# A hybrid decoder layer on one core: 128-row attention scores, both chunks of the triangular inverse doubled in common, and an instruction planner that prices row changes

## The chip, the cores and the metric

The kernel runs on one core of a Trainium2 chip. A time is what the device takes for one execution, in microseconds (us); the median over several executions counts. The profile comes from one more execution, whose own time stands beside its span. The engines are called PE (TensorE, matmuls), DVE (VectorE), ACT (ScalarE), POOL (GpSimd) and SP (SyncE, which issues the DMAs).

## The reference

One decoder layer, float32, 256 tokens of width 1024. `x` is RMS-normalised and multiplied by one weight matrix of 1024 x 4104. Half of the columns feed eight softmax heads of 64, the other half four heads of 128 of a gated delta rule; both results are gated, concatenated, multiplied by `w_out`, normalised and added to `x`:

```python
h = rms_norm(x, norm_pre_w)
a_q, a_k, a_v, a_z, d_q, d_k, d_v, d_z, d_b, d_a = split(h @ w_in)
moba_out = moba_attention(a_q, a_k, a_v) * silu(a_z)       # causal, ALiBi, 8 heads of 64
g_q, g_k, g_v = split(silu(causal_conv4(concat(d_q, d_k, d_v))))
o = gated_delta_rule(g_q, g_k, g_v, g, beta)               # 4 heads of 128
gdn_out = rms_norm(o, gdn_norm_w) * silu(d_z)
return x + rms_norm(concat(moba_out, gdn_out) @ w_out, norm_post_w)
```

In the delta rule each chunk of tokens needs the inverse of a unit lower triangular matrix, `(I + A)^-1`, where `A` holds products of keys times decays.

## The kernel before

**Tiling.** Tokens are two tiles of 128 (`t` = 0, 1; for the delta rule these are its two chunks). Every projection is a product of float32 split in two float32r parts (`hi`, `lo`), three matmuls in place of one: `hi*hi + hi*lo + lo*hi`. The transposed input is `hhi`, `hlo`. A weight group (`dk`, `dq`, `dv`, `av`, `aq`, `ak`, `az`; 512 columns) comes in two DMAs of 1 MB into four `raw` buffers; ACT writes `..._hi` (a copy that rounds), DVE writes `..._lo` (the subtraction); PE runs 96 matmuls on each group.

**The first stage, `dz`** (lines 427 to 441 and 629 to 641). `x` comes in four DMAs of half rows, the weights of `d_z`, `d_b`, `d_a` (520 columns) in four DMAs of two of the eight k-slices. `dz_piece(1)` multiplies the right 264 columns for all k-slices, then `dz_piece(0)` the left 256. `d_b` and `d_a` lead to the gates `bet`, `gneg`. `ps_warm` matmuls on zeros fill PE while nothing else can run (`WARM`, flagged `late`).

**The gates' decay matrices** (692 to 703). Per chunk a bank `ps_d` gets a mask (`ident16` times `far16`, bf16) and then, head by head, `gs` (DVE: `strl` times the head's gate) times `triu`, in float32.

**The inverse** (stages `inv` and `dbl`, 769 to 875). `bT` is the transposed `A` of four heads. Diagonal blocks of 16 are solved by a loop of 15 steps on DVE (`wprod`, `wc`) for both chunks together. `dbl` then goes from blocks of 16 to 32, 64 and 128. It holds the transposed inverse `wT` and the inverse `xX`. Per chunk and level PE makes `ps_y` (from `bT` and `xX`), ACT copies it to `yz`, PE makes `ps_w` (subtracted from `wT` by DVE) and, at the first two levels, `ps_x` (subtracted from `xX`). At level 32 these matmuls use 32 rows of the array, at level 64 they use 64, and `ps_x` at level 16 uses 64 and 32; `ps_y` and `ps_w` at level 16 use all 128.

**The recurrence** (`rec`, 906 to 959): for chunk 0 `ps_p` from `wT` and `vt`, the state `ps_S`, the output `ps_o`; then chunk 1 with the state (`ps_kS`, `ps_qS`, `ps_p`, `ps_o`). `mixd` transposes the result for the output projection.

**Attention** (979 to 1032). Per head the scores go into a bank `ps_s` of 128 + 256 columns: queries of tile 0 against keys of tile 0 in plain float32 (`qa`, `ka`), queries of tile 1 against all keys in three float32r matmuls (`qa_h`, `qa_l`, `ka_h`, `ka_l`). A head has 64 features, so these matmuls use 64 rows; two heads of a pair lie in the two halves. Softmax on DVE and ACT, `ps_pt` transposes, `ps_av` multiplies by the values.

**The order.** Nothing runs as written. Each call is recorded (`record`, 149) with its reads and writes and a modelled `cost` (197); `run` (227) plays a list schedule over the engines, eight rounds, and `emit` (348) issues each engine's instructions in that order. So each engine's queue is fixed in advance, and PE runs what stands next in its queue. What decides between ready operations is a rank, moved per stage by `LEAD`; `SLACK` is the window on PE in which the rank decides; `LAT` the time from one engine to another. The model before knows that a matmul may use fewer rows (`work`) but has no price for going from one row range to another.

Of the kernel before, what the change touches and what calls it, by code (L numbers as in the profile page):

```python
# [111 lines left out]
class Op:  # L112
    __slots__ = ("n", "eng", "call", "args", "kw", "cost", "table", "preds", "succs", "bufs", "start", "end", "pin", "late", "boost", "work", "load", "pass_", "stage")
# [10 lines left out]
class Plan:  # L124
# [24 lines left out]
    def record(self, eng, real, name, args, kw):  # L149
# [16 lines left out]
        op.work = op.load = op.pass_ = 0.0  # L166
        if eng == "pe":
# [5 lines left out]
            k = views[1].box[0][1] - views[1].box[0][0]  # L173
            op.work = k / P
# [22 lines left out]
    def cost(eng, name, views, kw):  # L197
# [26 lines left out]
        row = (v.box[-1][1] - v.box[-1][0]) * 4  # L224
        return max(400, (v.box[0][1] - v.box[0][0]) * v.size() * 4 / (240 if v.box[1][1] - v.box[1][0] == KT // 2 else 330))

    def run(self, rank, banks, reverse=False):
# [26 lines left out]
        table, load, last = None, 1.0, 0.0  # L254
        window, done, cold, share, self.low = 0, {}, True, 1.0, 1.0
        for _ in range(len(ops)):
            best = None
            for e, todo in ready.items():
                cand = []
                for op in todo:  # L260
                    t = max(at[op], free[e])
                    if e == "pe":
                        t = max(t, last + op.load)
                    else:
                        t = max([t] + [b.held for b in op.bufs if b.tag is None])
# [6 lines left out]
                if not cand:  # L272
# [3 lines left out]
                    (c for c in cand if c[0] <= t0 + (SLACK if e == "pe" else 1)),  # L276
                    key=lambda c: (-1e9 if c[1].pin else 1e9 if c[1].late else rank[c[1]] - c[1].boost 
# [101 lines left out]
LEAD = {"out0": 3258, "dk": 2097, "inv": -1876, "av": 6719, "out1": -9380, "att0": -470, "mixd": -508}  # L379
WARM = 36  # L380
# [3 lines left out]
def tile_hybrid(  # L384
# [44 lines left out]
    dz_raw = [plan.tile(sb, [P, KH, GROUP + 2 * HG], F32, f"raw_dz{i}", tag="raw", bufs=RAW_BUFS) for i in range(2)]  # L429
    HD = D // 2  # L430
    for t in range(NT):
        for c0 in (0, HD):
            SP.dma_start(xs[t][:, c0 : c0 + HD], x[0, t * P : (t + 1) * P, c0 : c0 + HD], pin=True)
        if t == 0:
            SP.dma_start(wcol, norm_pre_w[0].rearrange("(p kt) -> p kt", kt=KT), pin=True)
    for k in range(0, KT, 2):
        SP.dma_start(dz_raw[k // KH][:, k % KH : k % KH + 2, :], w_cols[:, k : k + 2, 3584:], pin=True)
# [170 lines left out]
    def token_piece(raw, n, name, fine):  # L608

        banks = [bank([P, n], f"ps_{name}_{t}") for t in range(NT)]  # L610
        kn = 2 if n > 2 * PIECE - 1 else KH
        for kg in range(0, KT, kn):
# [3 lines left out]
            for k in range(kn):  # L616
                for t in range(NT):
                    ts = slice(t * P, (t + 1) * P)
                    kt = kg + k
                    PE.matmul(banks[t], hhi[:, kt, ts], hi[:, k, :], start=(kt == 0), stop=False)  # L620
                    PE.matmul(banks[t], hhi[:, kt, ts], lo[:, k, :], start=False, stop=False)
                    PE.matmul(banks[t], hlo[:, kt, ts], hi[:, k, :], start=False, stop=(kt == KT - 1))
# [5 lines left out]

    def dz_piece(half):
        n = PIECE + 2 * HG * half  # L630
        banks = token_piece(lambda k, m: dz_raw[k // KH][:, k % KH : k % KH + m, PIECE * half : PIECE * half + n],
                            n, f"dz{half}", 2)
        for t in range(NT):
            if half:
                V.tensor_copy(ba[:, t, :], banks[t][:, PIECE:])
            A.activation(zt[t][:, 2 * half : 2 * half + 2, :].rearrange("p h d -> p (h d)"), banks[t][:, :PIECE], AF.Silu)

    plan.stage = "dz1"
    dz_piece(1)
    plan.stage = "dz0"  # L640
    dz_piece(0)


# [46 lines left out]
    PE.matmul(pc.rearrange("p t h -> p (t h)"), triu, gneg.rearrange("p t h -> p (t h)"), start=True, stop=True)  # L690
    A.activation(egc, pc, AF.Exp, scale=-1.0)
    for t in range(NT):
# [122 lines left out]

    for t in range(NT):
        ns = sl(f"ms{t}", HB, f"ns{t}")
        V.tensor_tensor(ns, bT[t], lvl.rearrange("p n two s -> p (n two s)")[:, None, :].to_broadcast(HB), OP.mult)
        yz = sl(f"yz{t}", HB, f"yz{t}")
        G.memset(yz, 0.0)  # L820
        py = bank([P, HG, 64], f"ps_y16_{t}")
        for h in range(HG):
            PE.matmul(py[:, h, :], ns[:, h, :], half_cols(xX[t], 0, h), start=True, stop=True)
        A.activation(half_cols(yz, 0).sized(256), py.rearrange("p h (n s) -> p h n s", n=n), AF.Copy)
        pw = bank([P, HG, 64], f"ps_w16_{t}")
        for h in range(HG):
            PE.matmul(pw[:, h, :], yz[:, h, :], half_cols(wT[t], 1, h), start=True, stop=True)

        px = bank([P, HG, 2 * BASE], f"ps_x16_{t}")
        for b, nb in ((0, 2), (4 * BASE, 1)):  # L830
            r = slice(b, b + 2 * BASE * nb)

            def first(m, h=slice(None)):
                v = m[r, h, r]
                if h == slice(None):
                    return v.rearrange("p h (n two s) -> p h n two s", n=nb, two=2)[:, :, :, 0, :].sized(HG * BASE * nb)
                return v.rearrange("p (n two s) -> p n two s", n=nb, two=2)[:, :, 0, :]

            for h in range(HG):
                PE.matmul(px[r, h, : BASE * nb], wT[t][r, h, r], first(yz, h), start=True, stop=True)  # L840
            x_ = first(xX[t])
            V.tensor_tensor(x_, x_, px[r, :, : BASE * nb].rearrange("p h (n s) -> p h n s", n=nb), OP.subtract)
# [4 lines left out]
    for t in range(NT):
        py = bank([P, HG, L], f"ps_y32_{t}")
        pw = bank([P, HG, L], f"ps_w32_{t}")
        px = bank([P, HG, L], f"ps_x32_{t}")  # L850
        yz = sl(f"yz{t}", [P, HG, L], f"yz32_{t}")
        halves = [(slice(b, b + L), slice(b + L, b + 2 * L)) for b in range(0, P, 2 * L)]
        for r1, r2 in halves:
            for h in range(HG):
                PE.matmul(py[r2, h, :], bT[t][r1, h, r2], xX[t][r1, h, r1], start=True, stop=True)
            A.activation(yz[r2], py[r2], AF.Copy)
        for b, (r1, r2) in enumerate(halves):
            for h in range(HG):
                PE.matmul(pw[r1, h, :], yz[r2, h, :], wT[t][r2, h, r2], start=True, stop=True)
            if b == 0:  # L860
                for h in range(HG):
# [281 lines left out]
```

## Time and profile before

| | |
|---|---|
| median of 3 runs | 182.91 us (182.87 to 187.65) |
| profiled execution, own time | 183.36 us |
| its span in the profile | 181.6 us, mean granted PE clock 0.988 |
| PE busy | 171.3 us, 1351 instructions |
| DVE, ACT, POOL busy | 134.5, 104.6, 16.7 us |
| DMA | 24.91 MB, 137 GB/s on the mean |

Times inside the profile count from the first instruction. Every row carries line 366, the helper that issues all operations, so groups are told apart by tile names, read as output<-inputs. A PE row gives a matmul's start and its duration with the pipeline's latency; the pace of a stream is the distance from start to start. A plain float32 matmul shows as two records (two passes), a float32r matmul or a transpose as one. Both types are written `f32` in PE rows.

### The profile page before, as it was taken

Reading aid. Unit: us, or ns where it says so; the run is one execution under the profiler, and the core shown is the slowest. Engines: PE = TensorE matmul, PEld = TensorE weight load, DVE = VectorE, ACT = ScalarE, POOL = GpSimd, SP = SyncE. Lnnn points to the kernel's source line nnn. Section 1 sums busy time; section 2 is a strip of 40 time slices with the busy share of each in tenths; the row PEclk is TensorE's granted clock in tenths of the full one; section 3 lists DMA queues with packets and bytes.
Section 4 is the critical chain, followed back from the end, with each engine's and each line's share of the span. In section 5 each row is a group of like instructions: output and inputs, shape, how many; then the busy total and the mean of one; then the engine's idle time right before and its main releaser. Section 6 shows DMA issues by size and latency. Waiting matters only on the chain.

```text
span 181.6 us, 3546 instructions
## 1 busy us (share of the span) xinstructions
PE 171.3 (94%) x1351; PEld 155.8 (86%) x1351; DVE 134.5 (74%) x343; ACT 104.6 (58%) x231; POOL 16.7 (9%) x52
## 2 busy tenths in 40 slices
PE   6897999999999999999999999999999999999950
PEld 3585999999999978999999888898899998888850
DVE  3485969998599998594997787889885467962452
ACT  4486797393972948446643837745283488841130
POOL 8700000000030000400000000000000460000110
PEclk9999999999999999999999999999999999999995
DMA  5659799909955450625693515000000005500033
GB/s 154 247 206 304 230 277 296 368 23 253 277 166 128 122 216 14 216 84 220 195 391 78 196 13 218 0 5 0 5 0 4 0 0 137 213 0 0 0 115 115
DMA packets 12549, 24.91 MB, mean 137 GB/s; under 512 B 709, under 2 KB 1014, under 8 KB 12534
## 3 DMA queue, kind: packets, MB, share of 16 engines
q1 hardware_dynamic: 12534, 24.71, 43.0%
q8 instruction: 10, 0.16, 0.3%
q14 instruction: 5, 0.04, 0.1%
HBM read 23.65 MB, written 1.05 MB: 136 GB/s over the span
## 4 chain that ended last, share of the span: by engine, by line
PE 81%; DMA 7%; issue 4%; ACT 2%; SPq 2%; DVE 1%; POOLq 0%; POOL 0%; DVEq 0%; ACTq 0%
PE ps_out L366 9%; PE ps_av L366 8%; PE ps_az L366 7%; PE ps_ak L366 7%; DMA raw_dz<-in_w_in_dram 7%; PE ps_aq L366 6%; PE ps_dk L366 6%; PE ps_dq L366 6%; PE ps_dv L366 5%; PE ps_dz L366 5%; PE ps_s L366 4%; PE ps_pt L366 2%; PE ps_gb L366 2%; PE ps_y L366 2%; PE ps_w L366 2%
## 5 line engine op out<-in xcount | busy, mean ns | idle before, releaser
L366 DVE TENSOR_TENSOR o_lo<-raw_o,o_hi 128x1024 fp32r<-128x1024 f32 x8 | 9.8, 1222 | 2.6 <-ACT o_hi L366 2.6
L366 PE MATMUL ps_dz<-dz_hi,hhi 128*128 128x264 f32 (+1 forms) x32 | 9.3, 294 | 0.8 <-ACT dz_hi L366 0.8
L366 PE MATMUL ps_dz<-dz_lo,hhi 128*128 128x264 f32 (+1 forms) x32 | 9.4, 296 | 0.6 <-DVE dz_lo L366 0.6
L366 ACT ACTIVATE att_y<-att_y,mx 128x128 f32<-128x128 f32 (+1 forms) x16 | 7.1, 446 | 4.8 <-DVE mx L366 4.6
L366 PE MATMUL ps_az<-hlo,az_hi 128*128 128x256 f32 x32 | 9.8, 305 | 0.0
L366 ACT ACTIVATE o_hi<-raw_o 128x1024 fp32r<-128x1024 f32 x8 | 8.4, 1054 | 2.1 <-PE ps_out L366 2.1
L366 PE MATMUL ps_ak<-hlo,ak_hi 128*128 128x256 f32 x32 | 9.6, 300 | 0.0
L366 PE MATMUL ps_az<-hhi,az_lo 128*128 128x256 f32 x32 | 9.6, 303 | 0.0
L366 PE MATMUL ps_az<-hhi,az_hi 128*128 128x256 f32 x32 | 9.6, 300 | 0.0
L366 PE MATMUL ps_ak<-hhi,ak_lo 128*128 128x256 f32 x32 | 9.4, 299 | 0.0
L366 PE MATMUL ps_ak<-hhi,ak_hi 128*128 128x256 f32 x32 | 9.4, 293 | 0.0
L366 PE MATMUL ps_dq<-hhi,dq_lo 128*128 128x256 f32 x32 | 9.2, 287 | 0.0
L366 PE MATMUL ps_dq<-hlo,dq_hi 128*128 128x256 f32 x32 | 9.2, 286 | 0.0
L366 PE MATMUL ps_dq<-hhi,dq_hi 128*128 128x256 f32 x32 | 9.2, 286 | 0.0
L366 PE MATMUL ps_aq<-hhi,aq_hi 128*128 128x256 f32 x32 | 9.1, 284 | 0.0
L366 PE MATMUL ps_aq<-hhi,aq_lo 128*128 128x256 f32 x32 | 9.0, 282 | 0.0
L366 PE MATMUL ps_dk<-hlo,dk_hi 128*128 128x256 f32 x32 | 9.0, 281 | 0.0
L366 PE MATMUL ps_dk<-hhi,dk_hi 128*128 128x256 f32 x32 | 9.0, 281 | 0.0
L366 PE MATMUL ps_dv<-hlo,dv_hi 128*128 128x256 f32 x32 | 9.0, 281 | 0.0
L366 PE MATMUL ps_dv<-hhi,dv_hi 128*128 128x256 f32 x32 | 9.0, 280 | 0.0
L366 PE MATMUL ps_dv<-hhi,dv_lo 128*128 128x256 f32 x32 | 8.9, 280 | 0.0
L366 PE MATMUL ps_aq<-hlo,aq_hi 128*128 128x256 f32 x32 | 8.9, 284 | 0.0
(262 smaller groups left out, 634.2 us busy)
## 6 DMA issues: line engine op xcount, KB each, us to landing
raw_o<-in_w_out_dram SPq DMA_DIRECT2D x4, 1024.0 KB, 5.2
raw_dz<-in_w_in_dram SPq DMA_DIRECT2D x4, 520.0 KB, 9.3
raw_dk<-in_w_in_dram SPq DMA_DIRECT2D x2, 1024.0 KB, 12.0
raw_dq<-in_w_in_dram SPq DMA_DIRECT2D x2, 1024.0 KB, 9.0
raw_dv<-in_w_in_dram SPq DMA_DIRECT2D x2, 1024.0 KB, 7.5
raw_av<-in_w_in_dram SPq DMA_DIRECT2D x2, 1024.0 KB
raw_aq<-in_w_in_dram SPq DMA_DIRECT2D x2, 1024.0 KB, 6.1
raw_ak<-in_w_in_dram SPq DMA_DIRECT2D x2, 1024.0 KB, 6.8
```

The costliest lines, as they stand in the source:

```text
L366: op.call(*args, **kw)
```

## The change

All parts are made at once.

- **Scores over 128 rows.** `qz[m]` holds a pair's queries, `hi` and `lo`, once with the other head's 64 rows zero for each head; both query tiles go in three float32r matmuls over 128 rows. `qa` and `ka` are gone; POOL writes the zeros.
- **Inverse.** Both chunks share tiles and banks at each level. `ps_x` is gone: `xX` is made from `wT` by a DVE transpose of 32 x 32 blocks (two more of 128 x 512, one of 32 x 256).
- **Gates.** `gs` is one DVE multiplication per chunk, followed by one float32 matmul of 512 columns, with the mask matmul behind it.
- **First stage.** `x` in two DMAs, the weights in eight of one k-slice; each pair of slices is split once, for all 520 columns, and used by both halves.
- **Planner.** It prices a change of row range at 90 ns (`SWITCH`), adds a `MARGIN` between engines, has new DMA prices, `LEAD` values and `WARM`. Its order is new throughout.

The diff, cut to its core:

```diff
@@ record / cost / run
+            op.rows = views[1].box[0]
-        return max(400, ... / (240 if v.box[1][1] - v.box[1][0] == KT // 2 else 330))
+        return max(400, n / (350 if v.box[-1][1] - v.box[-1][0] > 520 else 230))
-                t = max(t, p.end + self.LAT[a.eng][b.eng])
+                t = max(t, p.end + self.LAT[a.eng][b.eng]
+                        + (0 if a.eng == "pe" == b.eng else MARGIN[2 if a.eng == "dma" else 0 if b.eng == "pe" else 1]))
-                        t = max(t, last + op.load)
+                        t = max(t, last + op.load, free[e] + SWITCH * (op.rows != rows))
-                    (c for c in cand if c[0] <= t0 + (SLACK if e == "pe" else 1)),
+                    (c for c in cand if c[0] <= t0 + (SLACK + SWITCH if e == "pe" else 1)),
+SWITCH = 90
+BATCH = 0
+MARGIN = [411, 175, 0]
-LEAD = {"out0": 3258, "dk": 2097, "inv": -1876, "av": 6719, "out1": -9380, "att0": -470, "mixd": -508}
-WARM = 36
+LEAD = {"out0": 3258, "dk": 2097, "inv": -3594, "av": 2525, "dbl": -402, "out1": -1204, "att0": -470, "mixd": -508, "az": -1375}
+WARM = 48
@@ first stage
+    for t in range(NT):
+        SP.dma_start(xs[t], x[0, t * P : (t + 1) * P, :], pin=True)
+    for k in range(KT):
+        SP.dma_start(dz_raw[k // KH][:, k % KH, :], w_cols[:, k, 3584:], pin=True)
...
+    for q in range(KT // 2):
+        zh, zl = hl_tiles([P, 2, NZ], f"dz{q}")
+        for k in range(2):
+            split_into(dz_raw[2 * q // KH][:, 2 * q % KH + k, :], zh[:, k, :], zl[:, k, :])
+        for k in range(2):
+            for t in range(NT):
+                token_mms(z1[t], zh[:, k, PIECE:], zl[:, k, PIECE:], kt, t, st, sp)
+            for t in range(NT):
+                token_mms(z0[:, t, :], zh[:, k, :PIECE], zl[:, k, :PIECE], kt, t, ...)
@@ gates
-        PE.matmul(pd, ident16, far16[:, None, :].to_broadcast(HB), start=True, stop=False)
-        for h in range(HG):
-            V.tensor_scalar(gs[:, h, :], strl, gneg[:, t, h : h + 1], None, op0=OP.mult)
-            PE.matmul(pd[:, h, :], gs[:, h, :], triu, start=False, stop=h == HG - 1)
+        V.tensor_tensor(gs, triu[:, None, :].to_broadcast(HB), gneg[:, t, :, None].to_broadcast(HB), OP.mult)
+        PE.matmul(pd, strl, gs, start=True, stop=False)
+        PE.matmul(pd, ident16, far16[:, None, :].to_broadcast(HB), start=False, stop=True)
@@ dbl, level 32 (levels 16 and 64 likewise over NH = 8 heads)
+    for r1, r2 in halves:
+        for h in range(NH):
+            PE.matmul(py[r2, h, :], bTa[r1, h, r2], xXa[r1, h, r1], start=True, stop=True)
+        A.activation(yz[r2], py[r2], AF.Copy)
+    for b, (r1, r2) in enumerate(halves):
+        for h in range(NH):
+            PE.matmul(pw[r1, h, :], yz[r2, h, :], wTa[r2, h, r2], start=True, stop=True)
+        V.tensor_tensor(wTa[r1, :, r2], wTa[r1, :, r2], pw[r1], OP.subtract)
+        if b == 0:
+            V.transpose(xXa[r2, :, r1], wTa[r1, :, r2])
@@ attention
+    for q in qz[:3]:
+        for e in range(2):
+            G.memset(q[DA * (1 - e) : DA * (2 - e), :, e, :].bitcast(F32), 0.0)
+                A.activation(qh, ps[b, c, :], AF.Copy, scale=qs_)
+                V.scalar_tensor_tensor(ql, ps[b, c, :], qs_, qh, op0=OP.mult, op1=OP.subtract)
-                PE.matmul(ps_s[:, :P], qa[b, m, :], ka[b, m, :], start=True, stop=True)
-                PE.matmul(ps_s[:, P:], qh[b, m, :], kh[b, m, :], start=True, stop=False)
-                ...
+                for o, ts, ks in ((ps_s[:, :P], slice(0, P), slice(0, P)), (ps_s[:, P:], slice(P, T), slice(0, T))):
+                    PE.matmul(o, qh[:, ts], kh[:, m, ks], start=True, stop=False)
+                    PE.matmul(o, qh[:, ts], kl[:, m, ks], start=False, stop=False)
+                    PE.matmul(o, ql[:, ts], kh[:, m, ks], start=False, stop=True)
```

More of the change, by code (lines that the diff above doesn't have):

```diff
@@ L112 @@
 class Op:
-    __slots__ = ("n", "eng", "call", "args", "kw", "cost", "table", "preds", "succs", "bufs", "start", "end", "pin", "late", "boost", "work", "load", "pass_", "stage")
+    __slots__ = ("n", "eng", "call", "args", "kw", "cost", "table", "preds", "succs", "bufs", "start", "end", "pin", "late", "boost", "work", "load", "pass_", "stage", "rows")
 class Queue:
@@ L166, in record @@
         op.work = op.load = op.pass_ = 0.0
+        op.rows = None
         if eng == "pe":
@@ L171, in record @@
             op.pass_ = n / RATE.get(dt, 2.4) + 2.5
-            k = views[1].box[0][1] - views[1].box[0][0]
-            op.work = k / P
+            op.rows = views[1].box[0]
+            op.work = (op.rows[1] - op.rows[0]) / P
         op.preds, op.succs, op.bufs = {}, [], []
@@ L223, in cost @@
         v = views[0]
-        row = (v.box[-1][1] - v.box[-1][0]) * 4
-        return max(400, (v.box[0][1] - v.box[0][0]) * v.size() * 4 / (240 if v.box[1][1] - v.box[1][0] == KT // 2 else 330))
+        n = (v.box[0][1] - v.box[0][0]) * v.size() * 4
+        return max(400, n / (350 if v.box[-1][1] - v.box[-1][0] > 520 else 230))
     def run(self, rank, banks, reverse=False):
@@ L253, in run @@
         bank_free = [(0.0, i) for i in range(BANKS)]
-        table, load, last = None, 1.0, 0.0
+        table, load, last, rows = None, 1.0, 0.0, None
         window, done, cold, share, self.low = 0, {}, True, 1.0, 1.0
@@ L291, in run @@
             c = op.cost
+            if op.eng == "pe":
+                rows = op.rows
             if op.eng == "pe" and not reverse:
@@ L428, in tile_hybrid @@
     GROUP = 2 * PIECE
-    dz_raw = [plan.tile(sb, [P, KH, GROUP + 2 * HG], F32, f"raw_dz{i}", tag="raw", bufs=RAW_BUFS) for i in range(2)]
     HD = D // 2
+    NZ = GROUP + 2 * HG
+    dz_raw = [plan.tile(sb, [P, KH, NZ], F32, f"raw_dz{i}", tag="raw", bufs=RAW_BUFS) for i in range(2)]
     for t in range(NT):
[L432 to L437, printed above, removed]
+        SP.dma_start(xs[t], x[0, t * P : (t + 1) * P, :], pin=True)
+    SP.dma_start(wcol, norm_pre_w[0].rearrange("(p kt) -> p kt", kt=KT), pin=True)
+    for k in range(KT):
+        SP.dma_start(dz_raw[k // KH][:, k % KH, :], w_cols[:, k, 3584:], pin=True)
     SP.dma_start(sv[0:48, :], conv_w[0].rearrange("j (c p) -> (j c) p", p=P), pin=True)
@@ L457, in tile_hybrid @@
         PE.matmul(pz[:, :256], wz[:, :P], wz[:, :256], start=True, stop=True, late=True)
+    HB = [P, HG, P]
+    NH = NT * HG
+    HBB = [P, NH, P]
+    of_chunk = [slice(t * HG, (t + 1) * HG) for t in range(NT)]
+    yz16 = sl("yz", HBB, "yz")
     ident = const([P, P], "ident")
@@ L606, in proj_group, with token_mms, token_piece @@
         return pss
-    def token_piece(raw, n, name, fine):
+    def token_mms(o, hi, lo, kt, t, first, last):
+        ts = slice(t * P, (t + 1) * P)
+        PE.matmul(o, hhi[:, kt, ts], hi, start=first, stop=False)
+        PE.matmul(o, hhi[:, kt, ts], lo, start=False, stop=False)
+        PE.matmul(o, hlo[:, kt, ts], hi, start=False, stop=last)
+    def token_piece(raw, n, name, kn, fine):
         banks = [bank([P, n], f"ps_{name}_{t}") for t in range(NT)]
-        kn = 2 if n > 2 * PIECE - 1 else KH
         for kg in range(0, KT, kn):
@@ L617, in token_piece @@
                 for t in range(NT):
[L618 to L622, printed above, removed]
+                    token_mms(banks[t], hi[:, k, :], lo[:, k, :], kg + k, t, kg + k == 0, kg + k == KT - 1)
         return banks
@@ L627, in tile_hybrid @@
     ba = const([P, NT, 2 * HG], "ba")
[L629 to L641, printed above, removed]
+    z1 = [bank([P, PIECE + 2 * HG], f"ps_dz1_{t}") for t in range(NT)]
+    z0 = bank([P, NT, PIECE], "ps_dz0")
+    for q in range(KT // 2):
+        plan.stage = "dz"
+        zh, zl = hl_tiles([P, 2, NZ], f"dz{q}")
+        for k in range(2):
+            split_into(dz_raw[2 * q // KH][:, 2 * q % KH + k, :], zh[:, k, :], zl[:, k, :])
+        for k in range(2):
+            kt = 2 * q + k
+            st, sp = kt == 0, kt == KT - 1
+            for t in range(NT):
+                token_mms(z1[t], zh[:, k, PIECE:], zl[:, k, PIECE:], kt, t, st, sp)
+            for t in range(NT):
+                token_mms(z0[:, t, :], zh[:, k, :PIECE], zl[:, k, :PIECE], kt, t, st and t == 0, sp and t == NT - 1)
+    plan.stage = "dz"
+    for t in range(NT):
+        V.tensor_copy(ba[:, t, :], z1[t][:, PIECE:])
+        A.activation(zt[t][:, 2:4, :].rearrange("p h d -> p (h d)"), z1[t][:, :PIECE], AF.Silu)
+    A_ = [zt[t][:, 0:2, :].rearrange("p h d -> p (h d)") for t in range(NT)]
+    for t in range(NT):
+        A.activation(A_[t], z0[:, t, :], AF.Silu)
     vh = const([P, NT, HA * DA], "vh", F32R)
@@ L814, in half_cols, with head_cols @@
+    def head_cols(m, i, h):
         return m[:, h, :].rearrange("p (n two s) -> p n two s", n=n, two=2)[:, :, i, :]
+    nsa = sl("ms", HBB, "ns")
     for t in range(NT):
[L817 to L842, printed above, removed]
@@ L843, in tile_hybrid @@
-        hc = half_cols(wT[t], 1).sized(256)
-        V.tensor_tensor(hc, hc, pw.rearrange("p h (n s) -> p h n s", n=n), OP.subtract)
-    L = 2 * BASE
[L847 to L861, printed above, removed]
-                    PE.matmul(px[r2, h, :], wT[t][r2, h, r2], yz[r2, h, :], start=True, stop=True)
-                V.tensor_tensor(xX[t][r2, :, r1], xX[t][r2, :, r1], px[r2], OP.subtract)
-            V.tensor_tensor(wT[t][r1, :, r2], wT[t][r1, :, r2], pw[r1], OP.subtract)
@@ L865, in tile_hybrid @@
[L865 to L875 removed]
+        V.tensor_tensor(nsa[:, of_chunk[t], :], bT[t],
+                        lvl.rearrange("p n two s -> p (n two s)")[:, None, :].to_broadcast(HB), OP.mult)
@@ L878, in tile_hybrid @@
+    H = P // 2
+    yz = sl("yz", [P, NH, H], "yz64")
+    py = bank([P, NH, H], "ps_y64")
+    for h in range(NH):
+        PE.matmul(py[H:, h, :], bTa[:H, h, H:], xXa[:H, h, :H], start=True, stop=True)
+    A.activation(yz[H:], py[H:], AF.Copy)
+    pw = bank([P, NH, H], "ps_w64")
+    for h in range(NH):
+        PE.matmul(pw[:H, h, :], yz[H:, h, :], wTa[H:, h, H:], start=True, stop=True)
+    V.tensor_tensor(wTa[:H, :, H:], wTa[:H, :, H:], pw[:H], OP.subtract)
     plan.stage = "dq"
```

98 lines of the change are left out of this document (50 added, 48 removed).

## The prediction

> **What bounds the kernel now.** I read the page first, then the time by stretches, the chain that ended last, and the order of time on PE where row ranges mix. The page's busy times and the chain:
>
> ```profile
> PE 171.3 (94%) x1351; PEld 155.8 (86%) x1351; DVE 134.5 (74%) x343; ACT 104.6 (58%) x231; POOL 16.7 (9%) x52
> PE 81%; DMA 7%; issue 4%; ACT 2%; SPq 2%; DVE 1%; POOLq 0%; POOL 0%; DVEq 0%; ACTq 0%
> ```
>
> PE carries 81% of the chain. The table by stretches has the stretch in us and its length, then for PE, weight loads, DVE, ACT and POOL the busy time and the instructions, then granted clock, DMA share and GB/s:
>
> ```profile
> 10.00:18.36 8.36, 6.94 (x47) 5.48 (x44) 5.61 (x16) 6.15 (x17) 0.00 (x0) 1.00 0.78 261
> 18.36:25.40 7.04, 7.04 (x56) 6.87 (x57) 5.04 (x16) 6.00 (x12) 0.00 (x0) 1.00 0.84 243
> 25.00:40.00 15.00, 15.00 (x129) 15.00 (x128) 14.50 (x37) 10.52 (x16) 0.00 (x0) 1.00 0.80 252
> 102.00:152.60 50.60, 50.60 (x492) 45.37 (x491) 37.60 (x129) 29.38 (x86) 4.99 (x12) 1.00 0.09 26
> 152.60:175.20 22.60, 22.58 (x121) 19.19 (x120) 13.97 (x21) 10.46 (x18) 0.56 (x1) 1.00 0.25 85
> 175.20:181.60 6.40, 0.00 (x0) 0.00 (x0) 2.08 (x5) 0.47 (x2) 0.56 (x1) 0.66 0.23 82
> ```
>
> From 18.36 to 175.2 PE has practically no idle time in these rows. So the time is what comes before 18.36, plus PE's queue, plus a tail of 6.4 us that the change leaves alone. A part of the change counts by the PE time it removes, as long as DVE and ACT keep up. In the steady stream 15.00 us hold 129 matmuls, 0.116 us each; most are float32r ones of 256 columns. That is the yardstick.
>
> **First stage.** The chain up to 18.36 (start, length, what):
>
> ```profile
> 4.08 0.47 SPq L366
> 4.60 12.31 DMA raw_dz<-in_w_in_dram
> 16.93 0.65 ACT dz_hi L366
> 17.60 0.72 DVE dz_lo L366
> 18.36 1.02 PE ps_dz L366 x6
> ```
>
> The last weights land at 16.91, are split, and PE is busy from 18.36. What it then does until 25.4 is mostly `dz`: the rest of the right half and all 48 matmuls of the left, 7.0 us. The change lets the left half use each slice as it lands. Free PE time for that lies in the stretch 10 to 18.36: of 8.36 us, some 45 matmuls that are no filler take 45 x 0.12 = 5.4 us, so 2.9 us are open. That is the gain if `dk` follows at once, and it nearly can:
>
> ```profile
> L366 SPq DMA_DIRECT2D raw_dk<-in_w_in_dram x2: 398/465/532, 10.6 to 11.7; - x2
> DMA to landing us min/median/max: 10.0/12.0/14.0
> L366 DVE TENSOR_TENSOR dk_lo<-raw_dk,dk_hi x4: 1218/1222/1225, 24.7 to 29.5; 128x1024 fp32r<-128x1024 f32 x4
> ```
>
> The first half of `dk` is issued at 10.6 and lands at 20.6; its ACT copy, taken as long as the subtraction (1.22), ends by 21.8. PE reaches `dk` at 25.4 now, so the gain ends at 25.4 - 21.8 = 3.6 us. Against it stand eleven issues in place of nine, 2 x 0.47 = 0.9 us on the last landing, in part won back if `x` in whole rows comes faster. SP has nothing else to do then; the four small loads and `dk` shift with it. I take **-2.5 us**, from -3.6 to +0.9. The twelve further fillers yield to everything that is ready; I cost them at nothing, and if PE were behind them it is these:
>
> ```profile
> 3.28 3.75 PE L366 MATMUL ps_warm<-wz 128*128 128x256 bf16 x18
> ```
>
> 12 x 3.75/18 = 2.5 us at worst, which would just eat this term.
>
> **Scores.** Order of time on PE (start, length, instruction), one visit to 64 rows, then a place where two heads share one, then the last visit's start:
>
> ```profile
> 102.55 0.28 PE L366 MATMUL ps_ak<-hhi,ak_lo 128*128 128x256 f32 x1
> 102.75 0.48 PE L366 MATMUL ps_s<-ka,qa 64*128 64x128 f32 x2
> 103.17 0.39 PE L366 MATMUL ps_ak<-hhi,ak_hi 128*128 128x256 f32 x1
> 103.39 0.28 PE L366 MATMUL ps_ak<-hlo,ak_hi 128*128 128x256 f32 x1
> ...
> 115.73 0.49 PE L366 MATMUL ps_s<-ka,qa 64*128 64x128 f32 x4
> ...
> 125.12 0.49 PE L366 MATMUL ps_s<-ka,qa 64*128 64x128 f32 x2
> ```
>
> From 102.55 to 103.39 are 0.84 us for two matmuls of the stream (0.23) and a head's float32 product (two passes, 0.24): the visit itself cost 0.36 us, in and out. There are twelve such visits, the first at 102.75, the last at 125.12: 4.3 us. The own work of eight heads is 8 x (0.24 + 3 x 0.12) = 4.8 us. After, no visit is left. A head has three matmuls of 256 columns and three of 128. The last kind, float32r with 128 columns of weights, the trace doesn't show; its neighbours are float32 passes with 128 weight columns and float32r ones with 64:
>
> ```profile
> 140.84 1.06 PE L366 MATMUL ps_qS<-S,qT 128*128 128x128 f32 x8
> 141.73 1.06 PE L366 MATMUL ps_p<-vt,wT 128*128 128x128 f32 x8
> ...
> 147.79 0.22 PE L366 MATMUL ps_av<-att_pTh,vh 128*64 128x128 f32 x1
> 147.85 0.22 PE L366 MATMUL ps_av<-att_pTl,vh 128*64 128x128 f32 x1
> ```
>
> That is 0.89/8 = 0.11 and 0.06 us. I take 0.11, the row with as many weight columns: 8 x (3 x 0.12 + 3 x 0.11) = 5.5, or 4.3 by the other. So 4.3 visits + 4.8 - 5.5 = -3.6 us, bounded by -4.8; since some visits serve two heads at once I take **-3.4**. [...]
>
> **Inverse.** The same view, and the row of the tile that goes away:
>
> ```profile
> 121.18 1.11 PE L366 MATMUL ps_x<-yz,wT 64*64 64x32 f32 x16
> 122.22 0.27 PE L366 MATMUL ps_av<-att_pTl,vh 128*64 128x128 f32 x1
> ...
> 139.40 0.68 PE L366 MATMUL ps_w<-wT,yz 64*64 64x64 f32 x8
> L366 PE MATMUL ps_x<-yz,wT x48: 177/191/240, 121.2 to 136.4; 64*64 64x32 f32 x16, 32*32 32x16 f32 x16, 32*32 32x32 f32 x16
> ```
>
> `ps_x` of chunk 0 at level 16 takes 1.04 us, 2.1 for both chunks, and its way in 3 x 0.18 for three visits. The sixteen at level 32 lie in visits that stay, at about 0.03 us each: 0.5. The other visits are four per chunk (level 32 and 64, `ps_y` and `ps_w`), the last at 139.40; eight become four: 4 x 0.36 = 1.4. Sum **-4.5 us**; if the two halves of level 32 are visited apart, -3.8. DVE pays for it:
>
> ```profile
> L366 DVE STREAM_TRANSPOSE xX<-wT 128x512 f32<-128x512 f32 x2 | 1.4, 704 | 0.0
> L366 DVE TENSOR_TENSOR xX<-xX,ps_x 32x128 f32<-32x128 f32 x2 | 0.6, 280 | 0.7 <-PE ps_x L366 0.7
> ```
>
> Two more transposes of 0.70 and a small one, against six subtractions of at most 0.28 (1.7) and the longer instructions that replace pairs: about equal.
>
> **Gates and operands.** The float32 product of four heads becomes one of 512 columns: the same passes, so the same PE time, without the breaks between heads. The mask matmul moves:
>
> ```profile
> 2.47 1.01 PE L366 MATMUL ps_d<-far,ident 128*128 128x512 bf16 x2 [0.34 <-DVE far L366]
> L366 DVE TENSOR_SCALAR gs<-strl,gneg 128x128 f32<-128x128 f32 x8 | 2.1, 278 | 0.0
> ```
>
> These two matmuls go from idle time at 2.47 into the dense stretch: at most 1.0 us, I take 0.4 (twice 0.2, as 256 columns take half of that in the stream), against some four breaks of 0.1 saved: **0**, from -0.5 to +1.0. DVE: 2.1 us become two instructions of 128x512 (0.7 each). The scaled queries cost DVE and ACT eight instructions of 64x256 each in place of eight and six; between 0.3 and 0.5 us for one, +1 us on DVE. POOL's zeros lie under 91% idle time. One wait is new: the fourth pair of heads reuses the first pair's tile, so its copies, now done by 94, wait for the first pair's scores.
>
> ```profile
> L366 ACT ACTIVATE qa_h<-ps_aq,qscale x4: 347/355/362, 89.7 to 93.0; 128x128 fp32r<-128x128 f32 x4
> ```
>
> The first scores start at 102.75, so these copies move by some 10 us and hold one of eight PSUM banks that long; behind them on ACT and DVE stand splits and softmax. The plan knows this wait and can put them behind other work: nothing by itself, and part of the next term if not.
>
> **Order.** `MARGIN` makes the plan expect inputs 0.4 us late on PE; it can only save stalls, and the rows above leave almost none to save. New `LEAD` values move work within a queue that is always full; order alone then gains nothing, and the last output tile stays last. I cost both at nothing; what they can do badly is rival (c).
>
> **Cover.** Of 50.6 us in the stretch 102 to 152.6 the terms take 7.9; DVE's 37.6 would then fill 88%. In 25 to 40 it ran at 14.50 of 15.00 without PE losing anything, so zero is one end. But there the work was independent; here the doubling is a chain, and it now holds both chunks:
>
> ```profile
> L366 DVE TENSOR_REDUCE wc<-wprod x15: 171/229/289, 95.1 to 116.4; 128x8 f32<-128x16 f32 x1, 128x8 f32<-128x24 f32 x1, 128x8 f32<-128x32 f32 x1, 128x8 f32<-128x40 f32 x1
> 131.71 0.83 PE L366 MATMUL ps_p<-vt,wT 128*128 128x128 f32 x6
> 138.41 1.06 PE L366 MATMUL ps_kS<-S,kT 128*128 128x128 f32 x8
> L366 DVE SCALAR_TENSOR_TENSOR bT<-ps_kk,dd,dT x8: 321/342/348, 50.8 to 61.9; 128x128 f32<-128x128 f32 x8
> ```
>
> Chunk 0's first product starts at 131.71 and the state's use at 138.41: these 6.7 us lie beside chunk 1's doubling now and stand behind it later. The solve must therefore be done about that much earlier than 116.4. It can be: `bT` is complete at 62.3, and the loop's fifteen steps are spread over 21 us. I charge **+2.5 us**, nearer to zero than to 6.7, because the room is there.
>
> **Sum.** -2.5 - 3.4 - 4.5 + 0 + 2.5 = -7.9 us on the profiled execution's 183.4 (span 181.6 and 1.8 around it): 175.5. The median of the runs shown, 182.91, lies 0.45 below it, so the forecast is **175.0 us**.
>
> **Rivals.** (a) *DVE and the chain take PE's place.* Cover costs the full 6.7: -2.5 - 3.4 - 4.5 + 6.7 = -3.7, 179.2 us. For it: 88% on DVE; against: 97% was borne. (b) *The planner does not do what it says*: the 128-row matmuls pace like two passes, the merged doubling is cut up again by filler matmuls, so that its visits stay, and the first stage waits for eight small DMAs as long as before. What is left is `ps_x`, 2.1 + 0.5 us: 180.3. For it: nothing in this trace shows a 128-wide float32r pass or a visit of eight heads. Against: the visits of scores cannot come back at 128 rows, so all three failures are needed. (c) *The chain sets the end, slower.* `LEAD` pushes `inv` back by 3594 in place of 1876, by 1.7 us. If the solve ends no earlier than now, at 116.4 + 1.7, output waits for the doubling and then chunk 0's 6.7 us in series, and PE stands idle there: 182.9 + 6.7 + 1.7 - 2.5 (the first stage) = 188.8. It decides from the solve's end: at 112 it is about nothing, past 116 it is slower. The profile's tail shows what idling adds: the granted clock falls to 0.66 there. [...]
>
> **How the numbers follow.** Forecast 0.60 (171 to 178), (a) 0.23 (177 to 181), (b) 0.10, (c) 0.07. Two per cent, about what a measurement of this kernel can tell from no change, is 179.3 to 186.6. Faster: 0.60, and two thirds of (a): 0.76. Same: the rest of (a), and (b): 0.17 with rounding. Slower 0.07. The range, 171 to 181, holds the forecast, (a) and (b) and leaves out (c) and the last of each; its low end is the terms at their good ends (-3.6 - 4.8 - 4.5 - 0.5 with 1.5 of cover).
>
> **What would show it.** Right: no 64-row `ps_s`, about four to six visits of `ps_y` and `ps_w`, no `ps_x`; PE busy without gaps from about 20 us to the last `ps_out`, in about 7 us less; the last `wc` reduction before 110; float32r matmuls of 128x128 at 0.11. Wrong: PE gaps between `ps_w` and `ps_p` (a, c), `dk_lo` still at 24.7 or later (first stage), or the last slice of `raw_dz` landing after 17.8.

## The result and the profile after

The changed kernel takes 174.83 us in the median (174.23 to 174.90), against 182.89 of the kernel before in the same session: a ratio of 0.953, 95% interval 0.948 to 0.958. The forecast was 175.0. The profiled execution took 174.88 us, its span is 172.9, against 183.36 and 181.6. A ratio leaves out the executions that took over 1.5% longer than the kernel's fastest; where the granted clock is needed to follow a time, it is given.

The page of the kernel after, busy times and the chain:

```profile
PE 164.1 (95%) x1311; PEld 154.1 (89%) x1311; DVE 134.7 (78%) x330; ACT 108.8 (63%) x231; POOL 21.2 (12%) x58
PE 87%; POOL 5%; issue 4%; ACT 1%; DVE 1%; POOLq 0%; DVEq 0%
```

PE lost 7.2 us of busy time and carries even more of the chain; DVE is where it was. The 7% that DMA held in the chain, the last weights of `dz`, are gone; POOL, which had none of it, now holds 5%. The same stretches, columns as before:

```profile
10.00:18.36 8.36, 7.97 (x64) 7.65 (x64) 7.70 (x20) 8.36 (x24) 1.25 (x9) 1.00 0.72 245
18.36:25.00 6.64, 6.64 (x55) 6.32 (x55) 3.44 (x11) 4.50 (x9) 0.00 (x0) 1.00 0.75 241
102.00:144.00 42.00, 42.00 (x426) 41.18 (x426) 36.81 (x110) 28.88 (x81) 5.21 (x12) 1.00 0.15 52
144.00:166.60 22.60, 22.60 (x126) 19.47 (x124) 11.74 (x19) 9.27 (x18) 0.56 (x1) 1.00 0.27 94
```

PE has no idle time from 18.36 to the last output matmul. The last row is the output, cut to the same length as before; its first matmul starts at 143.68, 8.9 us earlier than before (152.56). DVE stands at 36.81 of 42.00, the 88% that the prediction worked out.

Rows of single tiles of the kernel after: shortest, median and longest duration in ns, first to last start, forms:

```profile
L372 DVE TENSOR_TENSOR dk_lo<-raw_dk,dk_hi x4: 1217/1220/1226, 23.6 to 29.5; 128x1024 fp32r<-128x1024 f32 x4
L372 ACT ACTIVATE dz_hi<-raw_dz x8: 622/659/713, 7.7 to 17.5; 128x520 fp32r<-128x520 f32 x8
L372 DVE TENSOR_REDUCE wc<-wprod x15: 161/221/288, 79.3 to 98.7; 128x8 f32<-128x16 f32 x1, 128x8 f32<-128x24 f32 x1, 128x8 f32<-128x32 f32 x1, 128x8 f32<-128x40 f32 x1
```

`dk` moves up by 1.1 us (24.7 to 23.6). The last slice of `raw_dz` is copied from 17.5, so it has landed before 17.8. The solve ends at 98.7 and not at 116.4. In the order of time on PE (start, duration) these are all the visits to 32 or 64 rows that are left after 60 us, four where I count 26 before (a step from 64 to 32 rows counted as a visit of its own), the last one shown up to its first six matmuls:

```profile
110.20 1.09 PE L372 MATMUL ps_y<-xX,bT 32*32 32x32 f32 x32
112.55 1.09 PE L372 MATMUL ps_w<-wT,yz 32*32 32x32 f32 x32
115.50 1.14 PE L372 MATMUL ps_y<-xX,bT 64*64 64x64 f32 x16
118.12 0.56 PE L372 MATMUL ps_w<-wT,yz 64*64 64x64 f32 x6
```

To find the 8.3 us by which the last `ps_out` starts earlier (174.90 to 166.57), I added up PE's time from start to start by output tile, idle time apart (counted from PE's first matmul):

| us on PE | before | after | difference |
|---|---|---|---|
| idle, all of it ahead of 20 us but for 0.2 in the kernel before | 2.80 | 1.67 | -1.1 |
| `hT`, `dz`, fillers | 21.95 | 21.55 | -0.4 |
| `ps_x` | 2.55 | 0 | -2.55 |
| `ps_s` | 6.36 | 5.75 | -0.6 |
| `ps_y`, `ps_w` | 7.28 | 7.59 | +0.3 |
| the seven projections and `ps_av`, among which the visits stood | 90.98 | 88.79 | -2.2 |
| `ps_d` | 2.34 | 1.96 | -0.4 |
| the rest (transposes, recurrence, output, and 1.1 us ahead of PE's first matmul) | 40.64 | 39.26 | -1.4 |

### The profile page after: what moved, and what is told of

Its sections match the earlier page's. It is cut to its first block, busy times and chain, and to the rows that moved or that the text cites. A ratio compares the mean times of both kernels' runs of the same rounds, so it can differ in the third digit from the quotient of the medians.

```text
span 172.9 us, 3465 instructions
## 1 busy us (share of the span) xinstructions
PE 164.1 (95%) x1311; PEld 154.1 (89%) x1311; DVE 134.7 (78%) x330; ACT 108.8 (63%) x231; POOL 21.2 (12%) x58
## 4 chain that ended last, share of the span: by engine, by line
PE 87%; POOL 5%; issue 4%; ACT 1%; DVE 1%; POOLq 0%; DVEq 0%
PE ps_out L372 10%; PE ps_av L372 9%; PE ps_az L372 7%; PE ps_dz L372 7%; PE ps_ak L372 7%; PE ps_dq L372 7%; PE ps_aq L372 7%; PE ps_dv L372 7%; PE ps_dk L372 7%; PE ps_s L372 3%; PE ps_y L372 2%; PE ps_w L372 2%; PE ps_gb L372 2%; PE ps_pt L372 2%; PE ps_d L372 1%
## 5 line engine op out<-in xcount | busy, mean ns | idle before, releaser
L372 PE MATMUL ps_aq<-hlo,aq_hi 128*128 128x256 f32 x32 | 9.6, 299 | 0.0
L372 PE MATMUL ps_warm<-wz 128*128 128x256 bf16 x48 | 8.3, 333 | 1.1 <-DVE wz L372 1.1
L372 PE MATMUL ps_ak<-hlo,ak_hi 128*128 128x256 f32 x32 | 9.0, 280 | 0.0
```

Of the source, the lines that this page charges most:

```text
L372: op.call(*args, **kw)
```

## The experiments

The theory is the prediction's: PE's queue sets the time, and each part counts by the PE time that it removes. Rivals: the chain over DVE and ACT stands in PE's place; the planner's numbers make the gain, not the parts. A third came up with the first experiments: the granted clock. The runs were made in several sessions. The fastest execution of the kernel before lay between 182.40 and 182.93 us in all of them, so half a microsecond between kernels of different sessions says nothing.

**One part undone, under the new planner numbers.** Each kernel puts one part back as it was (the edits of this section are shortened):

```diff
# u_scores: queries of 64 rows again
-for o, ts, ks in (tile 0, tile 1): three float32r matmuls on qz[m], 128 rows
+ps_s[:, :P] <- qa[b], ka[b] float32; ps_s[:, P:] <- qh, ql, kh, kl, 64 rows
# u_dbl: the doubling per chunk, ps_x on PE
-py = bank([P, NH, 64]); ...; transpose32(t)
+py = bank([P, HG, 64]); ...; px = bank(...); x_ = x_ - px
# u_first: dz_piece(1), dz_piece(0), x in half rows, dz in four DMAs
# u_gates: gs by head, four matmuls by triu, the mask matmul ahead of them
```

> The changed kernel with the 64-row scores of before put back (plain float32 for tile 0, three float32r matmuls for tile 1), planner and all else as changed. PE-queue theory: the visits come back, fewer than twelve since the planner now prices them; four visits would cost 1.4 us, twelve 4.3, less the 0.5 us by which the new matmuls are longer: 176 to 178.6 us against 174.8, and the twelve-visit end only if the planner's price does nothing. Rival (the gain is the planner's new order, the scores cost what they cost): within 0.5 us of 174.8.

Measured: 187.35 us, ratio to the kernel before 1.018 (1.010 to 1.025): slower than before any change. Stretches of it, with the granted clock third from the end:

```profile
115.89:119.30 3.41, 2.91 (x38) 2.04 (x38) 1.75 (x10) 2.26 (x9) 0.00 (x0) 1.00 0.00 0
119.30:136.37 17.07, 17.07 (x81) 13.16 (x82) 7.06 (x25) 5.24 (x14) 0.00 (x0) 0.50 0.01 1
136.37:184.15 47.78, 43.36 (x294) 39.01 (x294) 28.89 (x64) 23.20 (x59) 5.51 (x14) 1.00 0.16 55
```

For 17.07 us the clock stands at half, with PE busy throughout. The 3.41 us before hold 0.50 us of idle time and visits to few rows in quick succession; of 37 matmuls that start there, 31 use 32 or 64 rows. From the order on PE:

```profile
116.15 0.24 PE L372 MATMUL ps_w<-wT,yz 32*32 32x32 f32 x2
116.71 0.24 PE L372 MATMUL ps_w<-wT,yz 32*32 32x32 f32 x2
117.19 0.24 PE L372 MATMUL ps_w<-wT,yz 32*32 32x32 f32 x2
117.75 0.65 PE L372 MATMUL ps_w<-wT,yz 32*32 32x32 f32 x18
118.90 0.37 PE L372 MATMUL ps_w<-wT,yz 32*32 32x32 f32 x6 [0.50 <-DVE wT L372]
```

Half of 17.07 is 8.5 us (at 0.50 the matmuls of 512 columns of `ps_out` follow each other after 0.43 us in az_two, at 1.00 after 0.23 in the kernel before). The span grew by 13.3 (172.9 to 186.2), PE's idle time in it by 0.2 (8.8 to 9.0). What is left is 4.6 us of PE work, where the prediction's term has 3.4.

> The changed kernel with the doubling of before put back: chunk by chunk, ps_x on PE, two DVE transposes in place of five. PE-queue theory: ps_x (2.6 us) and up to seven more visits at 0.36 us return, 177.4 to 179.6 us. Rival (a chain of both chunks costs cover, so that splitting it wins some back): 174 to 176.

Measured: 185.51 in the one execution at full clock (0.998); the other three took 199.7 to 200.9 at 0.90. There is no ratio. Even 185.51 is 10.7 us above the full change, more than twice the term of 4.5.

> The changed kernel with the loads and the first stage of before (x in four pieces, weights in four, right half before left half). PE-queue theory: dz ends later by about 2 us, as the trace has it (last dz matmul that other work waits for at 23.7 against some 26), so 176.5 to 177.5 us. Rival (PE makes it up later, since DVE and not PE sets the stretch after 25): within 0.5 us of 174.8.

Measured: 178.42 us, ratio 0.961 (0.952 to 0.969), 176.91 and 177.00 in the executions at full clock (0.996 and 0.994), 2.1 us above the full change. The last `dz` matmul starts at 25.8 in place of 23.7. PE waits 0.4 us longer for `hT` (the two gaps below, against 1.29 and 0.39):

```profile
8.47 0.35 PE L372 MATMUL hT<-ident,x 128*128 128x128 f32 x1 [0.88 <-DVE x L372]
11.97 0.38 PE L372 MATMUL hT<-ident,x 128*128 128x128 f32 x1 [1.17 <-DVE hlo L372]
```

> The changed kernel with the gates of before: mask matmul first (in idle time), head by head on DVE and PE. The forecast costs this part at 0: 174.3 to 175.3 us. Rival (the float32 matmul of 512 columns with the mask behind it, 1.96 us of PE in one piece in the trace, costs PE time that was free before): 173.8 to 174.4, faster without the part.

Measured: 177.37 us, ratio 0.963 (0.958 to 0.968): 2.5 us for a part costed at nothing. The profile puts 0.97 of it ahead of the output (next row), and `dz` ends 1.8 us later; `ps_d` itself takes 0.55 us more on PE (2.51 for 1.96). Both expectations missed. The order changed around it; what moved it I did not settle.

```profile
146.64 0.50 PE L372 MATMUL ps_out<-o_hi,mixd_hi 128*128 128x512 f32 x1 [0.97 <-ACT mixd_hi L372]
```

Three of the four parts undone therefore cost more than their terms, and differently by part. The planner numbers are those of the whole change, and the order they make is another one for each of these kernels; so the next ones go back to the numbers of before.

**The planner's numbers.**

```diff
# p_old: all five parts, planner as before
-LEAD = {... "inv": -3594, "av": 2525, "dbl": -402, "out1": -1204, ... "az": -1375}
+LEAD = {... "inv": -1876, "av": 6719, "out1": -9380, ...}
-WARM = 48; SWITCH = 90; MARGIN = [411, 175, 0]; new DMA cost
+WARM = 36; SWITCH = 0; MARGIN = [0, 0, 0]; old DMA cost
# p_margin0: the full change with MARGIN = [0, 0, 0] alone
# u_scores_plan, u_dbl_plan: u_scores and u_dbl with p_old's numbers
```

> All five parts stay; only the planner's numbers are those of before (its lead times, 36 fillers, no price for a row change, no margin, the old DMA model). The prediction costed the order at nothing: by it the time stays at 174.8 us, from 174 to 176. A rival says the order is worth part of the gain, since undoing one part under the new numbers cost more than the part's own term: then it is 177 us or more, with PE gaps between 100 and 145 us. A third says the old numbers put the remaining small-row matmuls closer together or apart and so change the granted clock; then the clock leaves 0.98.

Measured: 176.13 us in the profiled execution, clock 0.990; the median of four is 178.74, the others at 177.33 (clock 0.979), 180.15 and 180.54 (0.961). By that one execution at full clock the order was worth 1.25 us, not nothing, and the five parts alone bring 7.1 us (183.2 before in the same session): the planner's numbers do not make the gain. Ahead of the last `ps_out` PE idles 3.50 us, where the table has 1.67. The largest of the gaps that the new order closed, in the order on PE:

```profile
16.34 0.26 PE L372 MATMUL ps_cols<-ident,sv 49*128 49x49 f32 x1 [0.92 <-DMA sv<-in_conv_w_dram]
111.64 0.24 PE L372 MATMUL ps_y<-xX,bT 32*32 32x32 f32 x2 [0.52 <-ACT yz L372]
113.66 0.31 PE L372 MATMUL ps_w<-wT,yz 32*32 32x32 f32 x4 [0.50 <-DVE wT L372]
```

> The 64-row scores of before, with all other parts of the change, but now under the planner's numbers of before. With the new numbers this kernel took 187.35 us and its clock stood at 0.5 for 17 us. If that loss is the clock, brought on by visits to few rows standing close together, then numbers that spread them as before keep the clock near 0.99, and the time is the queue's sum: 174.8 + 3.4 (the prediction's term) and what the order costs, 178 to 181. If it is the visits' own price under any order, it stays at 186 to 188. If the clock falls again, the order isn't what sets it.

Measured: 182.0 us, ratio 0.986 (0.982 to 0.990); 179.81 to 180.67 at a clock of 0.99 and more. Against 176.13 that is 3.7 to 4.5 for a term of 3.4. Over the ten executions of this one order the clock lies between 0.934 and 0.996, so the order alone does not set it. The profiled execution, at 183.45, shows a fall behind 3.41 us without any idle time, in which 19 of 25 matmuls use 32 or 64 rows:

```profile
122.73:126.14 3.41, 3.41 (x29) 2.36 (x25) 2.04 (x9) 1.48 (x5) 0.00 (x0) 1.00 0.02 5
126.14:132.97 6.83, 6.83 (x31) 5.73 (x31) 3.00 (x12) 1.89 (x6) 0.00 (x0) 0.50 0.00 0
```

> The doubling of before, each chunk by itself with ps_x on PE, all other parts of the change, under the planner's numbers of before. Beside the kernel with those numbers and all five parts (176.1 us at best, 178.7 in the median) the prediction's term of 4.5 us gives 180.6 at best and 183.2 in the median. If the merged doubling is worth more because fewer visits to few rows also protect the clock, the median lies beyond 185 and the granted clock falls below 0.98. If the two transposes on DVE cost what ps_x did, it is 176 to 179.

Measured: 180.84 us, ratio 0.986 (0.977 to 0.995); 180.46 to 180.92 at a clock of 0.99. That is 4.3 to 4.8 above 176.13, for a term of 4.5.

> All of the change except the margin: the planner no longer expects inputs 0.41 us late on PE and 0.175 elsewhere. The prediction costed the margin at nothing: 174.3 to 175.3 us. If it is what removes the half-microsecond gaps between ps_y, its copy and ps_w, these gaps come back between 110 and 120 us and the time is 175.5 to 177; and if such gaps beside visits to few rows bring the clock down, single executions reach 180.

Measured: 180.12 to 180.19 at full clock (0.988 to 0.997), ratio 0.980 (0.972 to 0.989), 5.3 us above the full change. In its profiled execution (184.02, 10.2 us at half clock) the solve ends at 109.1 in place of 98.7, the gaps between `ps_y` and `ps_w` are back, and PE idles 2.4 us after 20 us, where the full change idles none. That explains less than half of 5.3; the rest stays open. The value of the margin can't be read by itself: one number changed moves the whole order.

**Less PE work, more chain.**

```diff
# az_two: the output lacks az's hi times hlo
-PE.matmul(o, hi[:, k, cs], hlo[:, kt, :])
+if name != "az": PE.matmul(o, hi[:, k, cs], hlo[:, kt, :])
# x3_transpose
+for _ in range(3): V.transpose(xX[t], wT[t])
# az_two_norm: az_two, and the norm of the delta rule's output left out
-osq, om, of; o = o * of * zt by head
+V.tensor_tensor(o, o, zt[t], OP.mult)
# az_two_fill: az_two, and eleven useless matmuls ahead of ps_ot and ps_out
+PE.matmul(po[:, 0, :], ident, on[0][:, 0:2, :])   # 7; 4 more with on[1]
```

> The last projection az leaves out one of its three products, hi times hlo: 32 float32r matmuls of 256 columns fewer, and the output lacks that part. If PE's queue is the bound up to the output, as the prediction has it, the time falls by 32 x 0.116 = 3.7 us to about 171.1. If the doubling's chain has become the bound (rival a), nothing of it is gained: 174.5 to 175, and PE shows the 3.7 us as gaps.

Measured: 177.42 us, ratio 0.968 (0.965 to 0.972): 3.7 us of work less, 2.6 us more time, all four executions at a clock of 0.975 to 0.984. The order on PE ahead of the output, then the stretches:

```profile
142.41 0.33 PE L372 MATMUL ps_ot<-ident,o 128*128 128x128 f32 x1 [1.53 <-DVE o L372]
144.73 0.80 PE L372 MATMUL ps_out<-o_hi,mixd_hi 128*128 128x512 f32 x1 [1.06 <-ACT mixd_hi L372]
```

```profile
139.81:143.22 3.41, 1.88 (x15) 1.30 (x12) 2.73 (x7) 3.40 (x6) 0.88 (x2) 1.00 0.46 148
143.22:150.05 6.83, 5.77 (x15) 4.31 (x15) 4.26 (x6) 2.62 (x5) 0.00 (x0) 0.50 0.01 3
```

Output starts at 144.73 where the full change starts it at 143.68: the gated result of the delta rule is not there earlier. So under this planner PE's queue and this chain end together in the full change. With less PE work PE waits, and behind the wait the clock stands at half for 6.83 us.

> Each of the four DVE transposes of 128x512 is done three times: eight more instructions of about 0.7 us, 5.6 us more on DVE, all on the chain from the solve to the output. If PE's queue is the bound and the chain has room, the time stays within 1 us of 174.8. If DVE or the chain is the bound (rival a), it grows by 2.8 to 5.6 us, to 177.6 to 180.4.

Measured: 186.51 us, ratio 1.018 (1.014 to 1.022). Both expectations were far off. The stretches:

```profile
117.54:120.95 3.41, 2.91 (x43) 2.43 (x44) 1.87 (x5) 1.02 (x4) 0.00 (x0) 1.00 0.00 0
120.95:134.60 13.65, 13.65 (x83) 12.96 (x82) 7.69 (x26) 3.95 (x13) 0.00 (x0) 0.50 0.01 2
134.60:155.08 20.48, 18.52 (x161) 18.06 (x160) 15.28 (x41) 15.55 (x44) 4.84 (x12) 1.00 0.15 47
155.08:158.49 3.41, 3.41 (x10) 2.66 (x9) 2.33 (x4) 1.10 (x3) 0.00 (x0) 0.50 0.47 183
```

The span grew by 11.5 us (184.4). Of that 3.0 are idle time on PE (0.50 in the first row, 0.52 just before it, 1.96 in the third) and half of 13.65 + 3.41 is 8.5. The sum is the whole: 5 us of DVE work cost 3.0 in waits and 8.5 in clock.

> Leaves out az's hi times hlo product (32 matmuls, 3.7 us of PE) and the norm of the delta rule's output (eight ACT squares, POOL's power, six of eight DVE multiplications): the chain from the recurrence to the output becomes about 3 us shorter. If that chain stands right behind PE's queue and is what kept the 3.7 us from being gained, the time is now about 171.1, with no gap before the output. If PE's queue wasn't the bound at all, or the doubling sets the end, it stays at 174 or above.

Measured: 175.42 us, ratio 0.954 (0.946 to 0.963). The gaps ahead of the output are gone and the clock is full (0.992 to 0.997), but the 171.1 did not come. In the planner's new order the doubling stands in pieces, thirteen visits to few rows in place of four; four of them, in the order on PE:

```profile
116.68 0.31 PE L372 MATMUL ps_w<-wT,yz 32*32 32x32 f32 x4
117.17 0.24 PE L372 MATMUL ps_w<-wT,yz 32*32 32x32 f32 x2
117.72 0.24 PE L372 MATMUL ps_w<-wT,yz 32*32 32x32 f32 x2
118.55 0.31 PE L372 MATMUL ps_w<-wT,yz 32*32 32x32 f32 x4
```

Nine visits at the prediction's 0.36 us would be 3.2 of the 3.7 us taken away. Up to the last `ps_out` PE's time from start to start, idle time apart, is the same as in the full change (163.9 us for 163.8): its queue was the bound here, as full as before, with other things in it.

> The kernel without az's hi times hlo product (32 matmuls fewer, that part missing from the output) took 177.4 us: more than the full kernel, with PE idle for 1.53 and 1.06 us before the output projection and the clock at 0.5 for 6.8 us behind that. Now eleven useless float32 matmuls (2.6 us) are added that depend on the recurrence's result and so stand in that gap. If the idle time is what halves the clock, the clock stays at 1.0 and the time falls to 173.8 to 174.5 although PE has more to do. If the clock falls for another reason, or the chain alone sets the time, it stays at 177 or above.

Measured: 187.37 us, ratio 0.995 (0.987 to 1.003); 181.7 and 181.9 at full clock (0.996 and 0.997). Inconclusive: the fillers moved the planner's order, the doubling came later, and in the profiled execution a gap of 1.64 us ahead of `ps_ot` remained. The clock did not fall behind this gap, but 37 us earlier, to 0.50 from 118.39 to 135.46. Whether the gap brings the clock down in az_two is not shown.

## Why the prediction was right, and where it was not

- **What bounds the kernel:** right. PE's queue from about 20 us to the last output matmul; no idle time there after.
- **First stage, -2.5:** the sign was right, the size 1.0 too large. On PE it brought 1.5 (idle -1.1, own work -0.4), and `dk_lo` moved up by 1.1; undone it cost 2.1. The last slices land early enough, and the last `dz` matmul starts at 23.74. But then ten fillers stand in PE's queue among the first products of `dk`, whose `hi` copies for these ACT had done by 21.64:

```profile
19.63 2.01 ACT L372 ACTIVATE dk_hi<-raw_dk 128x1024 fp32r<-128x1024 f32 x2
23.87 0.72 PE L372 MATMUL ps_warm<-wz 128*128 128x256 bf16 x5
24.34 0.36 PE L372 MATMUL ps_dk<-hhi,dk_hi 128*128 128x256 f32 x1
24.66 0.72 PE L372 MATMUL ps_warm<-wz 128*128 128x256 bf16 x5
25.14 0.36 PE L372 MATMUL ps_dk<-hhi,dk_hi 128*128 128x256 f32 x1
```

  They hold PE for 0.95 us (23.87 to 24.34 and 24.66 to 25.14). The prediction let fillers yield to everything that is ready; in a queue fixed in advance these did not. That they are the missing 1.0 us no run tested.
- **Scores -3.4 and inverse -4.5:** `ps_x` as worked out (2.1 + 0.5; 2.55 measured). The scores' own work is 5.75 for a forecast of 5.5, with 0.12 for float32r matmuls of 128x128 (0.24 from 99.87 to 100.11 for one of these and one of the stream):

```profile
99.87 0.23 PE L372 MATMUL ps_s<-ka_h,qz 128*128 128x128 f32 x1
99.94 0.33 PE L372 MATMUL ps_ak<-hhi,ak_hi 128*128 128x256 f32 x1
100.11 0.28 PE L372 MATMUL ps_ak<-hlo,ak_hi 128*128 128x256 f32 x1
```

  I also counted the time of each visit, from the start of the matmul ahead of it to the start of the second one behind it, less the usual pace of these two. The twelve visits of the scores come to 9.1 us before, as the prediction had it (4.3 + 4.8), against 5.75 after: the 3.4 are there. The eleven of the inverse come to 8.5 and its four after to 4.9: 3.6, for a term of 4.5. By the table the two together brought 6.4 us (`ps_x`, `ps_s`, `ps_y`, `ps_w`, projections and rest); the 0.6 between stands in other work of the queue and is not explained. Undone one at a time under one set of planner numbers they cost 3.7 to 4.5 and 4.3 to 4.8, near their terms.
- **Gates and operands, 0:** -0.4 on `ps_d`. Undone, the gates cost 2.5, of which `ps_d` explains 0.55; the rest stays open. POOL's zeros were not all laid under idle time. The 91% is a mean over the kernel; in the first 10 us POOL's busy time grew from 7.09 to 9.06 us (fifth column, before and after). Two of the zeros stand there ahead of `rx` in its queue, for which the scaling of `x` waits. What that costs is not separated.

```profile
0.00:10.00 10.00, 7.75 (x40) 5.12 (x41) 4.48 (x16) 4.64 (x11) 7.09 (x35) 1.00 0.59 202
0.00:10.00 10.00, 7.60 (x47) 5.81 (x47) 5.15 (x15) 4.84 (x9) 9.06 (x31) 1.00 0.58 214
```

- **Order, 0:** wrong, it was worth 1.25 us by p_old's one execution at full clock, and more where the clock falls (177.33 to 180.54 us at 0.979 to 0.961).
- **Cover, +2.5:** wrong. In the full change there was no stall to charge; the solve ended 17.7 us earlier, and nearly so under the old numbers, so it wasn't `LEAD` that moved it. The merged doubling did: u_dbl_plan differs from p_old in the doubling alone, and there the solve ends 14.3 us later. First p_old, then u_dbl_plan:

```profile
L372 DVE TENSOR_REDUCE wc<-wprod x15: 163/221/281, 81.7 to 100.0; 128x8 f32<-128x16 f32 x1, 128x8 f32<-128x24 f32 x1, 128x8 f32<-128x32 f32 x1, 128x8 f32<-128x40 f32 x1
L372 DVE TENSOR_REDUCE wc<-wprod x15: 173/230/280, 95.1 to 114.3; 128x8 f32<-128x16 f32 x1, 128x8 f32<-128x24 f32 x1, 128x8 f32<-128x32 f32 x1, 128x8 f32<-128x40 f32 x1
```

  A part of the stall does show in p_old: 1.6 us of idle time on PE after 20 us, for 0.2 before, and none in the full change. So order and cover were not separate terms. The 2.5 charged too much cancel the 2.1 by which first stage, scores, inverse and gates fell short: -1.5 - 6.4 - 0.4 is -8.3 (the order's gain within it) where the sum had -7.9. That the forecast came out within 0.2 us is luck; the number was better than its terms.
- **Rivals:** (a) did not happen but stands directly behind PE, by az_two: another 3.7 us off PE brought nothing under this planner. (b) is refuted by the four visits and the 0.12 us. (c) did not decide, as the solve ended at 98.7. Its remark on the clock looks at idling alone and missed the danger: in u_scores the clock stood at 0.50 for 17.07 us with PE busy throughout. And in the tail of the kernel before, the clock stands at 1.00 up to 177.26 and at 0.50 from there, about 2 us after the last matmul, with PE busy for 1.34 of the 3.42 us ahead:

```profile
173.84:177.26 3.42, 1.34 (x12) 1.14 (x10) 1.77 (x7) 0.95 (x4) 0.56 (x1) 1.00 0.12 44
```

## What to carry to other kernels

Time the path from start to start on the bound engine, tile by tile: it told where the time went when undoing single parts, each of which makes the planner order everything anew, did not. Before counting a gain on PE, look for what ends at the same moment as its queue. And where matmuls on few rows stand close together, look at the granted clock in each stretch before explaining a difference by waits: in u_scores, by the estimate above, half clock makes 8.5 of the 13.3 us and PE's idle time 0.2.

## What was unexpected of the hardware

In these runs the granted clock fell to 0.50 behind stretches in which the profile shows PE busy. It fell after 3.41 us with 2.91 us busy in u_scores and x3_transpose, and with 3.41 busy in u_scores_plan; of the matmuls that start there, 31 of 37, 32 of 42 and 19 of 25 use 32 or 64 rows. It then stayed at 0.50 for 17.07, 13.65 and 6.83 us of full PE activity. The second fall in x3_transpose lasted 3.41 us (155.08 to 158.49); the three lengths are 5, 4 and 2 times that, and its distance from the first one, 34.13 us (120.95 to 155.08), 10 times. It and the fall in az_two came behind 3.41 us with 1.45 and 1.88 us busy, without any matmul on few rows.

What brings the clock down stays open. The clock held behind 3.41 us of p_old in which 49 of 59 matmuls use 32 rows, and behind 3.41 us of az_two_fill with less busy time than az_two's:

```profile
109.39:112.80 3.41, 2.89 (x62) 2.52 (x62) 2.36 (x9) 1.23 (x5) 0.00 (x0) 1.00 0.74 282
152.53:155.94 3.41, 1.77 (x14) 1.41 (x12) 1.72 (x4) 1.44 (x4) 1.30 (x3) 1.00 0.30 112
```

A busy PE in these rows also counts each matmul's latency (the one at 99.87 above has a duration of 0.23 us, and the next starts 0.07 after it), so short pauses around a visit need not show as idle time; whether the rows or these pauses bring the clock down, no experiment varied by itself. Why u_dbl took 185.51 us in one execution (0.998) and 199.7 to 200.9 in the others (0.90) is not shown either.
